# An expert loop on one core: VectorE alone splits the weights, conditional blocks get PSUM banks of their own, and token counts are read earlier

## The chip, the cores and the metric

The kernel runs on one NeuronCore of a Trainium2 chip. Its engines are TensorE (PE in the views; PEld is its weight load), VectorE (DVE), ScalarE (ACT), GpSimd (POOL) and the queue engine SyncE (SP). The metric is the device time of one execution in microseconds. It is taken from repeated runs; one further execution was recorded by the hardware profiler.

## What is computed

The program is two transformer blocks over 1024 tokens of width 1024. The first is a hybrid mixer with an MLP, the second a hybrid mixer with a mixture of experts, and only the mixture of experts is touched here. Each token chooses one of four groups and two of the four experts in it, so there are 16 experts and 2048 assignments, spread unevenly. All arithmetic of the experts is in float32:

```python
def expert_block(args):
    xb, e = args
    return (jax.nn.silu(xb @ w_gate[e]) * (xb @ w_up[e])) @ w_down[e]
...
out = jnp.zeros((n_tok, dm), ys.dtype).at[row_tok].add(ys)
```

`w_gate[e]` and `w_up[e]` are 1024x512, `w_down[e]` is 512x1024, so an expert has 6 MB of weights.

## The kernel before

**Precision by splitting.** Every float32 matrix that TensorE multiplies is cut into a high part (a cast to the fast format fp32r) and a low part (the value less the high part). A product is then three matmuls: high by high, high by low, low by high (`PASSES`, line 37; `products`, line 2071).

**The expert loop** is in `moe` (line 2007). The loop over `q` takes the 16 experts in a fixed order. An expert is three units `f`: f=0 and f=1 each compute one half of the gate and up products (`gate_up`), f=2 the down product (`down`). Tokens come in blocks of 128. Block b=0 always runs. Blocks b=1 and b=2 run inside `more` (lines 2123 and 2125) only if the expert's token count `c` is over 128 or 256; they reuse the weights already cut. More blocks than three go to `rest`, which this data does not enter. In the profiled execution the 16 experts run 3,1,1,1,3,2,1,1,2,1,1,1,2,2,1,1 blocks, 24 in all. I call them experts 1 to 16, and single-block, two-block and three-block experts.

**Weights.** SP loads 1 MB halves into seven `half` buffers (line 1998). One half is cut into two pieces `hl` of 128x1024 values, four pieces to a unit, twelve to an expert, in ten rotating buffers. A piece needs one cast on ScalarE (line 2052) and subtractions (line 2054). These are made in steps of half a piece: the cast and a 128x512 subtraction in one step, the second 128x512 subtraction in the next. The second subtraction of every other piece goes to GpSimd, so per expert VectorE makes 18 subtractions and GpSimd 6. The steps are called between the matmuls of block 0 of the unit before, so about six pieces are cut ahead.

**Activations.** Block b's tokens are gathered by GpSimd into `xg` (line 2030), turned by TensorE into `pl` (line 2040) and split by ScalarE and VectorE into `xT` (lines 2044 and 2045). A gate/up result in PSUM goes through a tanh on ScalarE (line 2085) and two operations on VectorE (lines 2086 and 2087) into `et`. TensorE turns `et` (line 2093), and lines 2095 and 2096 split it into `ehT`, the input of `down`. The results of `down` are copied to `yo` by ScalarE (line 2112) and VectorE (line 2113) and scattered by GpSimd (line 2115). Within `down` of block 0, TensorE also turns block 0 of the next expert.

**What sets the order.** The loop is under a manual schedule: each engine executes its instructions in the order in which the code was written, and in that order alone. PSUM tiles `pd` come from one pool of four rotating banks, used by conditional and unconditional blocks alike. A tile that a conditional block may have used is released when the reading engine has passed the branch, whether the block ran or not.

At the end of an expert every engine reads the next count and branches:

```python
if q < 15:
    c = count(q + 1)
    more(c, turn)
```

Of the kernel before, what the change touches and what calls it, by code (L numbers as in the profile page):

```python
# [44 lines left out]
class Kern:  # L45
# [1961 lines left out]
    def moe(s, hn_d, y_d):  # L2007
# [5 lines left out]
        with s.pool("me") as pl:  # L2013
# [12 lines left out]

            def fetch(e, b, full=False, to=None):

                o = 8 * e + b
                nc.gpsimd.indirect_dma_start(  # L2030
                    out=XG[b if to is None else to], out_offset=None, in_=hn_d,
                    in_offset=bass.IndirectOffsetOnAxis(ap=(ifull if full else ia)[:, o:o + 1], axis=0),
                    **({} if full else dict(bounds_check=T - 1, oob_is_err=False)))
# [13 lines left out]
            def split_of(x):  # L2047


                w = pl.tile([128, 2, 2, 512], F32R, name="hl", tag="hl", bufs=s.B_HL)  # L2050
                W.append(w)
                nc.scalar.copy(w[:, 0], x)  # L2052
                for i in range(2):
                    (nc.gpsimd if i and len(W) % 2 == 0 else V).tensor_sub(  # L2054
                        w[:, 1, i], x[:, i], w[:, 0, i].bitcast(F32))
                    if i == 0:
                        yield

            def cuts():

                while True:
                    n = len(W)
                    if n >= 192:
                        while True:
                            yield
                    yield from split_of(s.halves[n // 2][:, n % 2 * 2:n % 2 * 2 + 2])
                    yield
# [6 lines left out]
            def gate_up(b, w, f, step=lambda: None):  # L2074

                ps = s.psd()
                step()
                for k in range(8):
                    products(ps, XT[b][:, :, k], w, k, k == 0, k == 7)
                    if f == 1 and k == s.LEAD:  # L2080
                        turned(b, 0)
                    if k < 7:
                        step()
                g, x, t = ps[:, :256], ps[:, 256:], ET[b]
                nc.scalar.activation(t, g, AF.Tanh, scale=0.5)
                V.scalar_tensor_tensor(t, t, 1.0, g, op0=OP.add, op1=OP.mult)
                V.scalar_tensor_tensor(t, t, 0.5, x, op0=OP.mult, op1=OP.mult)
# [10 lines left out]
            def down(b, w, e, o, step=lambda: None, between=()):  # L2098

                Q = [s.psd(), s.psd()]  # L2100
                between = list(between)
                step()
                for n, (k, nh) in enumerate(((0, 0), (1, 0), (0, 1), (1, 1), (2, 0), (3, 0), (2, 1), (3, 1))):
                    products(Q[nh], EH[b][:, :, k], w, 2 * k + nh, k == 0, k == 3)
                    if n == s.T_B:
                        turned(b, 1)
                    if n > s.LEAD and between:
                        between.pop(0)()
                    if n < 7:
                        step()  # L2110
# [17 lines left out]
            def rest(q, b, c):  # L2128
# [3 lines left out]
                with tc.If(c > 128 * b):  # L2132
# [3 lines left out]
                    for f in range(3):  # L2136
                        w = []
                        for r in range(2):
                            x = s.half(e, f, r)
                            for i in range(2):  # L2140
                                s.run(split_of(x[:, 2 * i:2 * i + 2]))
                                w.append(W.pop())
# [7 lines left out]
            cut = cuts()  # L2150
            step = lambda: next(cut)
            with tc.manual_schedule(engines={POOL, PE, ACT, DVE}):
# [6 lines left out]
                for n in range(2 * (s.B_HL - 4)):  # L2159
                    step()  # L2160
                for q in range(16):
                    e = ORDER[q]
                    nxt = [lambda: turn(0, (0,)), lambda: turn(0, (1,))] if q < 15 else ()
                    for f in range(3):
# [10 lines left out]
                        if f < 2:  # L2175
                            more(c, lambda b: gate_up(b, w, f))
                        else:
                            more(c, lambda b: down(b, w, e, b))
                    if q < 15:
                        c = count(q + 1)  # L2180
                        more(c, turn)
# [96 lines left out]
```

## Time and profile before

| | us |
|---|---|
| median of 3 runs | 3620.5 (3619.45 to 3627.08) |
| the profiled execution | 3621.05 |
| its span, first to last instruction | 3619.2 |
| TensorE busy | 3371.8 (93% of the span) |
| VectorE busy | 2188.0 (60%) |
| ScalarE busy | 1197.8 (33%) |
| GpSimd busy | 897.1 (25%) |
| the expert loop in it | about 3028 to 3549, some 521 |

Nearly all of the program is bound by TensorE; the page's 40 slices show it 9 tenths busy or more in most of them, and lower ones in the last eight, where the expert loop lies. An engine's busy time does not tell by itself who waits for whom, so the rows used below are timelines of single experts and tables of waits. A timeline row is the start, the duration, the engine with the line, the operation, out and in, and the count of instructions merged into it; in brackets stands how long the engine was idle before and what ended that.

### The profile page before, as it was taken

Reading aid. Unit: us, or ns where it says so; the run is one execution under the profiler, and the core shown is the slowest. Engines: PE = TensorE matmul, PEld = TensorE weight load, DVE = VectorE, ACT = ScalarE, POOL = GpSimd, SP = SyncE. Lnnn points to the kernel's source line nnn. Section 1 sums busy time; section 2 is a strip of 40 time slices with the busy share of each in tenths; the row PEclk is TensorE's granted clock in tenths of the full one; section 3 lists DMA queues with packets and bytes.
Section 4 is the critical chain, followed back from the end, with each engine's and each line's share of the span. In section 5 each row is a group of like instructions: output and inputs, shape, how many; then the busy total and the mean of one; then the engine's idle time right before and its main releaser. Section 6 shows DMA issues by size and latency. Waiting matters only on the chain. (4 is left out here: it accounts for less than half of the span.)

```text
span 3619.2 us, 53008 instructions
## 1 busy us (share of the span) xinstructions
PE 3371.8 (93%) x20364; PEld 2907.8 (80%) x20364; DVE 2188.0 (60%) x4131; ACT 1197.8 (33%) x2013; POOL 897.1 (25%) x785
## 2 busy tenths in 40 slices
PE   7899999999999999999999999999999998898882
PEld 6889988899998998989977788888877786676671
DVE  5846666575566756666646844444556377757764
ACT  4433232322323223232333222222335333535552
POOL 1325223143232432323330000000120113524532
PEclk9999999999999999999999999999998998999995
DMA  3121111111121212111131221111252236847745
GB/s 102 55 61 44 50 41 50 47 43 51 49 56 36 52 42 58 45 47 43 53 136 63 82 70 48 49 47 47 82 148 70 75 111 228 272 164 240 265 165 200
DMA packets 311761, 324.60 MB, mean 90 GB/s; under 512 B 59340, under 2 KB 265784, under 8 KB 310800
## 3 DMA queue, kind: packets, MB, share of 16 engines
q1 hardware_dynamic: 245168, 258.53, 22.5%
q10 hardware_dynamic: 55936, 45.13, 4.4%
q0 software_dynamic: 10368, 17.10, 1.4%
q8 instruction: 180, 2.95, 0.3%
q14 instruction: 109, 0.89, 0.1%
HBM read 294.87 MB, written 46.47 MB: 94 GB/s over the span
## 5 line engine op out<-in xcount | busy, mean ns | idle before, releaser
L76 PE MATMUL pd<-wh,hT 128*128 128x256 f32 x6144 | 817.2, 289 | 1.9 <-DVE tg L600 1.9
L76 PEld LDWEIGHTS pd<-wh,hT 128*128 128x128 f32 x6144 | 768.0, 194 | 11.1 <-issue 2.7
L160 ACT CAST wh<-wr 128x512 fp32r<-128x512 f32 (+1 forms) x417 | 250.6, 601 | 941.6 <-PE pd L76 570.8
L76 PE MATMUL pd<-hT,wh 128*128 128x512 f32 x2256 | 562.0, 399 | 0.0
L161 DVE TENSOR_TENSOR wh<-wr,wh 128x512 fp32r<-128x512 f32 (+1 forms) x417 | 296.8, 718 | 414.9 <-ACT wh L160 413.6
L76 PEld LDWEIGHTS pd<-hT,wh 128*128 128x128 f32 x2256 | 413.6, 189 | 80.9 <-issue 0.2
L1171 PE MATMUL pd<-wh,uT 128*128 128x512 f32 x1536 | 360.2, 393 | 2.9 <-DVE acc L1179 1.9
L76 PE MATMUL pd<-h2T,wh 128*128 128x512 f32 x1536 | 352.8, 390 | 0.0
L1171 PEld LDWEIGHTS pd<-wh,uT 128*128 128x128 f32 x1536 | 286.9, 188 | 70.1 <-DVE acc L1179 8.3
L76 PEld LDWEIGHTS pd<-h2T,wh 128*128 128x128 f32 x1536 | 287.8, 188 | 60.5 <-issue 0.2
L2071 PE MATMUL pd<-hl,xT 128*128 128x512 f32 x1152 | 293.7, 413 | 30.6 <-DVEq L2123 23.3
L2071 PEld LDWEIGHTS pd<-hl,xT 128*128 128x128 f32 x1152 | 225.3, 200 | 89.1 <-ACT hl L2052 21.7
L2054 DVE TENSOR_TENSOR hl<-half,hl 128x512 fp32r<-128x512 f32 x288 | 259.0, 944 | 31.6 <-ACT hl L2052 26.7
L1179 DVE TENSOR_TENSOR acc<-acc,pd 128x512 f32<-128x512 f32 x224 | 146.8, 686 | 99.4 <-PE pd L1171 99.0
L2052 ACT CAST hl<-half 128x1024 fp32r<-128x1024 f32 x192 | 191.5, 1048 | 20.9 <-ACTq L2123 12.1
L2054 POOL TENSOR_TENSOR hl<-half,hl 128x512 fp32r<-128x512 f32 x96 | 139.4, 1462 | 222.0 <-ACT hl L2052 200.5
L1099 POOL TENSOR_TENSOR acc<-acc,gain 128x1024 f32<-128x1024 f32 x8 | 21.3, 2667 | 563.2 <-ACT hr L1098 563.1
L2071 PE MATMUL pd<-hl,ehT 128*128 128x512 f32 x576 | 151.5, 406 | 7.1 <-DVE ehT L2096 3.6
L76 PE MATMUL pd<-h3T,wh 128*128 128x512 f32 x552 | 140.1, 412 | 6.8 <-ACT bx L1457 5.5
L598 POOL TENSOR_SCALAR tg<-tg 128x256 f32<-128x256 f32 x96 | 86.1, 897 | 213.2 <-ACT tg L597 155.2
L135 POOL TENSOR_TENSOR orr<-orr,mhalf 128x4 f32<-128x4 f32 (+1 forms) x48 | 50.4, 1050 | 346.4 <-DVE orr L134 346.1
L76 PEld LDWEIGHTS pd<-h3T,wh 128*128 128x128 f32 x552 | 106.8, 196 | 35.3 <-ACT bx L1457 6.1
(582 smaller groups left out, 4934.5 us busy)
## 6 DMA issues: line engine op xcount, KB each, us to landing
wr<-in_w_in_dram SPq DMA_DIRECT2D x392, 128.0 KB, 2.3
half<-in_expert_w_gate_dram SPq DMA_DIRECT2D x64, 512.0 KB, 4.3
half<-in_expert_w_up_dram SPq DMA_DIRECT2D x64, 512.0 KB, 5.6
half<-in_expert_w_down_dram SPq DMA_DIRECT2D x32, 1024.0 KB, 5.0
wr<-in_w_up_dram SPq DMA_DIRECT2D x64, 256.0 KB, 2.7
wr<-in_w_down_dram SPq DMA_DIRECT2D x64, 256.0 KB, 2.5
wr<-in_w_in_dram SPq DMA_DIRECT2D x56, 256.0 KB, 2.8
x_d<-xr SPq DMA_DIRECT2D x16, 512.0 KB, 2.6
```

The lines of the kernel that those rows point to most:

```text
L76: return s.nc.tensor.matmul(out, a, b, start=start, stop=stop, **kw)
L135: nc.gpsimd.tensor_tensor(out, out, s.mhalf[:, :n], op=OP.pow)
L160: s.nc.scalar.copy(wv[:, 0], rv)
L161: s.nc.vector.tensor_sub(wv[:, 1], rv, wv[:, 0].bitcast(F32))
L598: nc.gpsimd.tensor_scalar(t[:, :, 128:], t[:, :, 128:], 1.0, None, op0=OP.add)
L1099: nc.gpsimd.tensor_mul(row, row, gpost)
L1171: nc.tensor.matmul(ps, ups[fb][k][:, a, t * 128:(t + 1) * 128], p[k][:, b, 0, :], start=(n == 0), stop=(n == 6 * len(fbs) - 1))
L1179: nc.vector.tensor_add(o, o, ps)
L2052: nc.scalar.copy(w[:, 0], x)
L2054: (nc.gpsimd if i and len(W) % 2 == 0 else V).tensor_sub(w[:, 1, i], x[:, i], w[:, 0, i].bitcast(F32))
L2071: nc.tensor.matmul(ps, lhs[:, a], w[i // 2][:, c, i % 2], start=first and n == 0, stop=last and n == 2)
```

## The change

Three edits, all in the expert loop.

1. **Subtractions.** A step is now a whole piece: one cast of 128x1024 and one subtraction of 128x1024 on VectorE. GpSimd makes none. Four steps fall into a unit, before every second product group. Twelve subtractions per expert replace 18 on VectorE and 6 on GpSimd.
2. **Banks.** The pool's four `pd` banks are taken once and given fixed parts, with the banks `ps` and `pt` besides. Block 0 uses banks 0 and 1 for gate/up and 2 and 3 for down. Conditional blocks use 4 and 5 only.
3. **Counts.** The next expert's count is read after unit f=0. The conditional turning of the next expert's blocks 1 and 2 stands before the conditional `down` blocks of this expert, no longer after them.

```diff
+            BANKS = [s.psd() for _ in range(4)] + [s.pss(), s.pst()]
...
                 w = pl.tile([128, 2, 2, 512], F32R, name="hl", tag="hl", bufs=s.B_HL)
-                W.append(w)
                 nc.scalar.copy(w[:, 0], x)
-                for i in range(2):
-                    (nc.gpsimd if i and len(W) % 2 == 0 else V).tensor_sub(
-                        w[:, 1, i], x[:, i], w[:, 0, i].bitcast(F32))
-                    if i == 0:
-                        yield
...
+                V.tensor_sub(w[:, 1], x, w[:, 0].bitcast(F32))
+                return w
+
+            def step():
+
+                n = len(W)
+                if n < 192:
+                    W.append(split_of(s.halves[n // 2][:, n % 2 * 2:n % 2 * 2 + 2]))
...
-                ps = s.psd()
-                step()
+                ps = BANKS[f] if b == 0 else BANKS[3 + b]
                 for k in range(8):
+                    if k % 2 == 0:
+                        step()
                     products(ps, XT[b][:, :, k], w, k, k == 0, k == 7)
...
-                Q = [s.psd(), s.psd()]
+                Q = BANKS[2:4] if b == 0 else BANKS[4:6]
...
+                    if n % 2 == 0:
+                        step()
                     products(Q[nh], EH[b][:, :, k], w, 2 * k + nh, k == 0, k == 3)
...
-                for n in range(2 * (s.B_HL - 4)):
+                for n in range(s.B_HL - 4):
                     step()
...
                             more(c, lambda b: gate_up(b, w, f))
+                            if f == 0 and q < 15:
+                                c1 = count(q + 1)
                         else:
+                            if q < 15:
+                                more(c1, turn)
                             more(c, lambda b: down(b, w, e, b))
-                    if q < 15:
-                        c = count(q + 1)
-                        more(c, turn)
+                    c = c1
```

On TensorE, at the end of expert 2, the kernel before has the last `down` matmuls of block 0, the conditional `down`, the count, the conditional turning and the next expert's first matmul (`pd` with a number is a PSUM tile, `ehT1` and `xT0` are the inputs of block 1 and block 0):

```order
L2071 MATMUL pd_27540<-hl_27427,ehT0_26764 128x512 x3
L2123 COMPARE_AND_BRANCH
L2071 MATMUL pd_27612<-hl_27331,ehT1_26765 128x512 x3
...
L2123 UNCONDITIONAL_BRANCH
L2149 TENSOR_LOAD cnt_26700
L2123 COMPARE_AND_BRANCH
L2040 MATMUL pl_27700<-ident_86,xg1_26759 128x128 x4
...
L2071 MATMUL pd_27738<-hl_27442,xT0_26761 128x512 x6
```

With the change the same place reads:

```order
L2064 MATMUL pd_26775<-hl_27004,ehT0_26764 128x512 x3
L2114 COMPARE_AND_BRANCH
L2042 MATMUL pl_27178<-ident_86,xg1_26759 128x128 x4
...
L2114 COMPARE_AND_BRANCH
L2064 MATMUL ps_26776<-hl_26891,ehT1_26765 128x512 x3
...
L2114 UNCONDITIONAL_BRANCH
L2064 MATMUL pd_26772<-hl_27018,xT0_26761 128x512 x6
```

The turning moved ahead of the conditional `down`, the count is gone from here, and the conditional block now writes `ps_26776` and `pt_26777` while the next expert's first product has a bank of its own, `pd_26772`.

On VectorE, in units f=1 and f=2 of block 0 of an expert, the conditional parts left out, the kernel before has:

```order
L2054 TENSOR_TENSOR hl<-half,hl 128x512 x3
L2086 SCALAR_TENSOR_TENSOR et_26767<-et_26767,pd 128x256
L2087 SCALAR_TENSOR_TENSOR et_26767<-et_26767,pd 128x256
...
L2054 TENSOR_TENSOR hl<-half,hl 128x512 x2
L2096 TENSOR_TENSOR ehT_26764<-pl,ehT_26764 128x256
L2054 TENSOR_TENSOR hl<-half,hl 128x512 x2
L2045 TENSOR_TENSOR xT_26761<-pl,xT_26761 128x512
L2054 TENSOR_TENSOR hl<-half,hl 128x512
L2045 TENSOR_TENSOR xT_26761<-pl,xT_26761 128x512
L2054 TENSOR_TENSOR hl<-half,hl 128x512
L2113 COPY yo_26770<-pd 128x512
```

With the change:

```order
L2053 TENSOR_TENSOR hl<-half,hl 128x1024 x2
L2078 SCALAR_TENSOR_TENSOR et_26767<-et_26767,pd 128x256
L2079 SCALAR_TENSOR_TENSOR et_26767<-et_26767,pd 128x256
...
L2053 TENSOR_TENSOR hl<-half,hl 128x1024
L2088 TENSOR_TENSOR ehT_26764<-pl,ehT_26764 128x256
L2053 TENSOR_TENSOR hl<-half,hl 128x1024 x2
L2047 TENSOR_TENSOR xT_26761<-pl,xT_26761 128x512 x2
L2053 TENSOR_TENSOR hl<-half,hl 128x1024
L2104 COPY yo_26770<-pd 128x512
```

The operations on `et`, `ehT`, `xT` and `yo` keep their places; the subtractions between them became fewer and wider, and the two on `xT` are now back to back. ScalarE's row of casts is the same in both kernels.

## Rows read from the trace of the kernel before

**Rows 1.** Waits of TensorE in the loop: us in total, times, longest.
```profile
PE pd L2071 <- DVEq L2123: 23.3, 9, 2.9
PE pl L2093 <- DVEq L2123: 12.3, 9, 1.9
PE pl L2040 <- DVEq L2123: 7.3, 3, 2.8
```

**Rows 2.** Stretch table, nine single-block experts with a successor: columns, one, sum.
```profile
core 0: us, PE busy (x) PEld busy (x) DVE busy (x) ACT busy (x) POOL busy (x), PEclk, DMA share, GB/s
...
3134.59:3159.11 24.52, 20.37 (x84) 15.48 (x85) 19.23 (x27) 13.49 (x18) 13.18 (x10) 0.92 0.96 314
...
sum 222.30, PE 178.88 PEld 135.66 DVE 180.81 ACT 132.96 POOL 115.39; mean PE 19.88 PEld 15.07 DVE 20.09 ACT 14.77 POOL 12.82
```

**Rows 3.** TensorE's timeline: end of expert 3, start of 4; expert 7 from 3255.72.
```profile
3130.08 1.64 PE L2071 MATMUL pd<-hl,ehT 128*128 128x512 f32 x6
3134.59 10.47 PE L2071 MATMUL pd<-hl,xT 128*128 128x512 f32 x36 [2.87 <-DVEq L2123]
...
3255.72 5.69 PE L2071 MATMUL pd<-hl,xT 128*128 128x512 f32 x24 [1.95 <-DVEq L2123]
...
3270.96 0.41 PE L2093 MATMUL pl<-ident,et 128*128 128x128 f32 x2 [1.68 <-DVEq L2123]
...
3274.78 1.64 PE L2071 MATMUL pd<-hl,ehT 128*128 128x512 f32 x6
3279.29 5.71 PE L2071 MATMUL pd<-hl,xT 128*128 128x512 f32 x24 [2.87 <-DVEq L2123]
```

**Rows 4.** VectorE's timeline at the end of expert 3 and start of 4.
```profile
3131.58 0.68 DVE L2045 TENSOR_TENSOR xT<-pl,xT 128x512 fp32r<-128x512 f32 x1
3132.18 1.61 DVE L2054 TENSOR_TENSOR hl<-half,hl 128x512 fp32r<-128x512 f32 x1
3133.71 0.68 DVE L2113 COPY yo<-pd 128x512 f32<-128x512 f32 x1
3135.33 3.72 DVE L2054 TENSOR_TENSOR hl<-half,hl 128x512 fp32r<-128x512 f32 x6 [0.94 <-ACT hl L2052]
```

**Rows 5.** GpSimd's timeline there: a subtraction, and a gather's descriptors.
```profile
3131.98 1.26 POOL L2054 TENSOR_TENSOR hl<-half,hl 128x512 fp32r<-128x512 f32 x1 [2.08 <-ACT hl L2052]
...
3138.44 1.47 POOL L2030 DMA_INDIRECT xg<-hn_d,ia  x1 [0.31 <-issue]
```

**Rows 6.** Stretch table of line 2054 alone, the same nine experts: sum.
```profile
sum 222.30, DVE 145.69 POOL 77.55; mean DVE 16.19 POOL 8.62
```

**Rows 7.** Line 665 by source, a 128x1024 operation of VectorE: ns min/median/max.
```profile
L665 DVE TENSOR_TENSOR aq<-aq,af x8: 1206/1213/3432, 96.5 to 1600.6; 128x1024 f32<-128x1024 f32 x8
```

**Rows 8.** Line 2149 by source, TensorE's queue reading a count: ns min/median/max.
```profile
L2149 PEldq TENSOR_LOAD <-cnt x16: 302/310/1162, 3021.7 to 3525.2; - x16
```

**Rows 9.** Stretch table, the four two-block experts: the sum.
```profile
sum 162.18, PE 149.57 PEld 118.92 DVE 94.89 ACT 72.74 POOL 59.15; mean PE 37.39 PEld 29.73 DVE 23.72 ACT 18.19 POOL 14.79
```

**Rows 10.** TensorE's timeline: start of expert 5; two-block expert 14; start of expert 16.
```profile
3159.11 1.94 PE L2040 MATMUL pl<-ident,xg 128*128 128x128 f32 x8 [2.82 <-DVEq L2123]
...
3163.28 20.29 PE L2071 MATMUL pd<-hl,xT 128*128 128x512 f32 x84
...
3463.43 1.06 PE L2040 MATMUL pl<-ident,xg 128*128 128x128 f32 x8 [1.43 <-DVEq L2125]
3465.03 11.17 PE L2071 MATMUL pd<-hl,xT 128*128 128x512 f32 x48 [0.53 <-ACT xT L2044]
...
3497.01 4.37 PE L2071 MATMUL pd<-hl,ehT 128*128 128x512 f32 x18
...
3527.91 8.59 PE L2071 MATMUL pd<-hl,xT 128*128 128x512 f32 x24 [2.87 <-DVEq L2123]
```

**Rows 11.** The load queue SP in the loop: its longest wait; landing times of halves.
```profile
SPq L1998 <- DVE hl L2054: 310.7, 75, 13.4
...
DMA to landing us min/median/max: 3.3/5.0/10.2
```

More of the change, by code (lines that the diff above doesn't have):

```diff
@@ L2050, in split_of @@
                 w = pl.tile([128, 2, 2, 512], F32R, name="hl", tag="hl", bufs=s.B_HL)
-                W.append(w)
                 nc.scalar.copy(w[:, 0], x)
-                for i in range(2):
-                    (nc.gpsimd if i and len(W) % 2 == 0 else V).tensor_sub(
-                        w[:, 1, i], x[:, i], w[:, 0, i].bitcast(F32))
-                    if i == 0:
-                        yield
[L2059 to L2067, printed above, removed]
+                V.tensor_sub(w[:, 1], x, w[:, 0].bitcast(F32))
[4 more added lines that the diff above has]
+                    W.append(split_of(s.halves[n // 2][:, n % 2 * 2:n % 2 * 2 + 2]))
             def products(ps, lhs, w, i, first, last):
@@ L2081, in gate_up @@
                         turned(b, 0)
-                    if k < 7:
-                        step()
                 g, x, t = ps[:, :256], ps[:, 256:], ET[b]
@@ L2098, in down @@
             def down(b, w, e, o, step=lambda: None, between=()):
-                Q = [s.psd(), s.psd()]
+                Q = BANKS[2:4] if b == 0 else BANKS[4:6]
                 between = list(between)
-                step()
                 for n, (k, nh) in enumerate(((0, 0), (1, 0), (0, 1), (1, 1), (2, 0), (3, 0), (2, 1), (3, 1))):
+                    if n % 2 == 0:
+                        step()
                     products(Q[nh], EH[b][:, :, k], w, 2 * k + nh, k == 0, k == 3)
@@ L2108, in down @@
                         between.pop(0)()
-                    if n < 7:
-                        step()
                 yo = YO[b % 2]
@@ L2139, in rest @@
                             x = s.half(e, f, r)
-                            for i in range(2):
-                                s.run(split_of(x[:, 2 * i:2 * i + 2]))
-                                w.append(W.pop())
+                            w += [split_of(x[:, 2 * i:2 * i + 2]) for i in range(2)]
                         if f < 2:
@@ L2149, in moe @@
             count = lambda q: nc.values_load(s.cnt[0:1, ORDER[q]:ORDER[q] + 1], min_val=0, max_val=1024)
-            cut = cuts()
-            step = lambda: next(cut)
             with tc.manual_schedule(engines={POOL, PE, ACT, DVE}):
```

## The prediction

> **What bounds the kernel now.** The change lies in the expert loop, about 521 of 3619 us. The chain of waits that ended last covers only the last 40 us, behind the loop, and tells nothing of it. So I read first TensorE's waits in the loop, then the loop expert by expert in the stretch table, then the timelines of the engines around one wait.
>
> The waits [rows 1] have one releaser, VectorE's queue passing the branch at line 2123: 23.3 us before an expert's first product, 7.3 us before the turning at its start, 12.3 us before the transposes in `down`. They belong to the single-block experts. Ten of 16 are such, and the nine with a successor take 222.30 us, 24.70 each, with TensorE busy 19.88 and VectorE 20.09 [rows 2]. Neither engine is full: they wait for each other in turn. A two-block expert needs twice the products for the same weights, and there VectorE is well ahead.
>
> One seam shows how. TensorE ends expert 3 at 3131.72 and starts expert 4 at 3134.59 [rows 3]. What the first product reads was ready earlier: the last subtraction on `xT` ended at 3132.26. VectorE still made a subtraction until 3133.79 and the copy of `yo` until 3134.39, then passed the branch [rows 4]. So TensorE waited for a bank that a conditional block, which did not run, might have used. That subtraction took 1.61 us where the others take 0.62 from start to start (3.72 for six), since GpSimd subtracted at the same time [rows 4, 5].
>
> The clock follows. The start of expert 4, behind 2.87 us of idleness, shows 36 products in 10.47 us; expert 7, with no dip behind its 1.95 us, 24 in 5.69, which would be 8.6 for 36 [rows 3]. Expert 4's granted clock is 0.92 [rows 2], so part of it ran at 1.2 GHz, the rest at 2.4. Not every long gap is followed by a dip (expert 8 starts with 24 in 5.71 behind 2.87 [rows 3]).
>
> **The banks, for a single-block expert.** TensorE's own work is read from expert 7: 3255.72 to 3276.42 at full clock is 20.70, less its wait of 1.68 in `down`, 19.02 [rows 3]. Of the 2.87 at the seam there remain the branches and what is left until `xT` is split, 0.54 in expert 3 (3131.72 to 3132.26) for its second half, which the first product does not need; I take 0.3. TensorE alone would then need 19.3. The Trainium skill (Perfetto Trace Analysis, Optimization Strategy) says that the same gap repeating on the engine that should be full can mean too little SBUF or PSUM for the next tile. Read so, the whole 2.87 would go and the expert would take 19.0 at best, 2.7 us less over nine; the rows keep the 0.3.
>
> **The subtractions.** VectorE is busy 20.09 us in such an expert, 16.19 of it in 18 subtractions [rows 2, 6]; 3.90 is other work and stays. The trace has no 128x1024 subtraction into fp32r, the nearest is line 665: median 1.213 us, slowest 3.432 [rows 7]. I take the median, because with GpSimd's subtractions gone nothing shown here disturbs it: a gather's descriptors on GpSimd (3138.44) left the six subtractions beside them at 0.62 [rows 4, 5]. Back to back they overlap by some 0.06 (0.68 long, 0.62 apart), so twelve cost 12 x 1.15 = 13.8. With 3.9 that is 17.7; empty stretches at branches, the count read (0.31, as on TensorE's queue [rows 8]) and waits for a cast add 1.0 to 1.5: 18.7 to 19.2. ScalarE's work, 14.77 [rows 2], is unchanged and stays hidden. GpSimd keeps only gathers and scatters.
>
> Both engines now need about 19.3. They still meet once per expert: the `et` of f=1 must be ready when six `down` products are done, and it stands behind up to one whole subtraction, 1.2 us long and no longer 0.68. The wait there is 12.3 over nine today, 1.37 each [rows 1]; with VectorE no longer behind I leave 0.5. So 19.8 per expert, a saving of 24.70 - 19.8 = 4.9, nine times: **44.1 us**. No dip is left in this number; today's dips are within the 24.70.
>
> **The other experts.** Two-block expert 14 at full clock took 36.35 from its first product to its end (3465.03 to 3501.38) [rows 10]. With 0.3 of branches it is 36.65, and 1.1 more for turning block 1 (1.06) where that lies in its stretch, which is so in three of four: 4 x 36.65 + 3 x 1.1 = 149.9, against 162.18 [rows 9]: **12.3 us**. The gap behind such an expert goes for the same reason. Three-block expert 5 spends 4.17 us (3159.11 to 3163.28) on turning 16 tiles that cost 1.06 per eight at full clock; with the gap ahead of it gone: **2.1 us**. Expert 1 starts cold and does not change. The last expert's first unit, 8.59 for 24 products against 5.69: **2.9 us** [rows 3, 10].
>
> **The count and the turning.** The count read moves from a place where TensorE waited anyhow to one behind a running unit; it costs at most 0.31 x 15 = 4.7 us if nothing hides it, and I take 0, since the queue reads ahead of the running products. It must be below the 0.3 that I leave at each seam to matter. Behind the moved turning the conditional `down` is queued on TensorE; the turning needs `pl` tiles that VectorE frees with `xT`, a wait of some 0.5 at six experts at most, and its gather is as old as before. It counts within the 1.1. At the loop's start the first subtraction is 1.21 instead of 0.69 long: 0.5 lost.
>
> **Sum.** 44.1 + 12.3 + 2.1 + 2.9 - 0.5 = 60.9 us. The profiled execution took 3621.05, so 3621.05 - 60.9 = 3560.15, **3560**. The median of the runs is 0.55 lower, which I neglect.
>
> **Rivals.**
>
> *VectorE stays behind.* The wider subtraction delays whatever stands behind it: the 1.37 in `down` stay and grow by 1.21 - 0.68 = 0.53 to 1.9, and the 0.54 for `xT` stays. Then 19.0 + 0.3 + 1.9 + 0.5 = 21.7, a saving of 3.0 x 9 = 27.0 and with the other 16.8 together 43.8: **3577**. For it: the two engines are level in my sum, so any slip falls on TensorE. Against: VectorE loses 2.4 us of work per expert (16.19 - 13.8). The Trainium skill (Perfetto Trace Analysis, Optimizing Scalar/DVE Operations) speaks for this rival: where VectorE is not full but causes bubbles elsewhere, its instructions should be broken up; this change does the opposite.
>
> *The loads become the bound.* In expert 4 the DMA engines were busy 0.96 and moved 314 GB/s [rows 2], so full they would move some 327. A single-block expert needs 6.3 MB of weights, 0.5 of tokens, 0.5 of results: 7.3 MB, 22.4 us. Saving 2.3 x 9 + 16.8 = 37.5: **3584**. Against: SP waits 310.7 us for VectorE to free a buffer, and a half lands within 10.2 us [rows 11], while seven halves, more than one expert's six, lie ahead; three single-block experts in a row would fall behind by 3 x 2.6 = 7.8 us and live off that lead. The Trainium skill (DMA: Bandwidth & Descriptors, Specifications) gives about 358 GB/s as a core's limit from HBM; by it an estimate is 20.4 us per expert, 18 us better over nine than by the row.
>
> *The banks free nothing*, because something else in VectorE's queue holds TensorE at the seam. Only the subtractions' 2.4 x 9 = 21.6 are won: **3599**.
>
> *Slower.* The disturbance of VectorE is not GpSimd's subtraction but something that stays. At each of the 12 places the wide subtraction then costs twice the 1.61 of [rows 4], 3.2 us, near the slowest of line 665, 3.43 [rows 7]: 12 x 3.15 + 3.9 + 1.3 = 43.0 per single-block expert, 18.3 x 9 = 165 lost, 16.8 won: **3769**. It decides from 24.70 + 16.8/9 = 26.6 per expert, that is a subtraction of 1.84 us. Against: the undisturbed six beside the gathers.
>
> **Chances.** Forecast 0.62; VectorE behind 0.17; loads 0.09; banks free nothing 0.06; slower 0.06. What a measurement can tell from no change is about 0.2%, 7 us. Faster by more than that take the first three cases and part of the fourth: 0.90; within it 0.04; slower 0.06. The range: at best TensorE alone bounds the single-block experts and the seam costs nothing, 19.0, which saves 0.8 x 9 = 7.2 more, 3553, with 3 us for what else is small: 3550. Above it reaches over the first two rivals, to 3586.
>
> **What would show it.** Right: TensorE's waits for VectorE's branch ahead of line 2064's first product near zero; single-block experts at 19 to 20.5 us; granted clock 1.00 in them; wide subtractions at 1.21 us with nothing on GpSimd beside them. Wrong: wide subtractions of 1.5 us and more; a wait before the transposes in `down` of 1.5 us or more in every single-block expert; ScalarE waiting for landing halves in the third of a row of single-block experts; dips that stay without the seam's gap.

## The result and the profile after

The changed kernel takes 3572.0 us (median of 4 runs, 3570.4 to 3578.0) against 3620.6 for the kernel before: 48.6 us less, ratio 0.9865 with a 95% interval of 0.9848 to 0.9882. The forecast was 3560, in a range of 3550 to 3586. So the sign and the range held, and the size was 12 us too large.

The profiled execution took 3570.43 us (span 3568.6), 50.6 less than the one of before. Read by the loop alone, from the first product of expert 1 to the last of expert 16, it is 518.3 us before (3030.42 to 3548.73) and 471.4 after (3027.63 to 3499.05): 46.9 less. The other 3.7 lie outside the loop, where nothing was changed: the loop of these profiles starts anywhere between 3025 and 3035. The loop's length is the steadier measure, and the same kernel profiled again gave 470.6. I use it below; but each is the loop of one execution, and a difference of 1 us tells nothing.

TensorE's waits in the loop, us in total, times, longest. The 23.3, 12.3 and 7.3 of [rows 1] have gone. What is left is mostly short gaps behind branches, 29 of them adding up to 16.8 us (the first three rows), and 3.3 us in all before the transposes in `down`:

```profile
PE pd L2064 <- PEq L2114: 8.6, 15, 0.8
PE pd L2064 <- PEq L2116: 4.9, 8, 0.8
PE pd L2064 <- ACTq L2116: 3.3, 6, 0.8
PE pl L2085 <- DVEq L2114: 3.3, 13, 0.4
```

The stretch table, columns as in [rows 2]: two of the nine single-block experts with a successor and the sum of the nine, the sum of the four two-block experts, and the loop as one stretch. The stretches are laid as in [rows 2, 9]; a conditional turning counts to the stretch in which it stands, so that for expert 14 now counts to expert 13, and that for expert 6 to expert 5, as before:

```profile
3103.56:3123.88 20.32, 18.74 (x84) 14.34 (x85) 18.20 (x22) 14.89 (x20) 5.84 (x4) 1.00 0.98 326
3123.88:3143.45 19.57, 18.59 (x85) 14.44 (x85) 17.73 (x21) 14.14 (x19) 5.83 (x4) 1.00 1.02 357
...
sum 180.93, PE 168.18 PEld 129.42 DVE 158.36 ACT 129.96 POOL 51.48; mean PE 18.69 PEld 14.38 DVE 17.60 ACT 14.44 POOL 5.72
...
sum 158.67, PE 146.84 PEld 114.82 DVE 93.24 ACT 72.67 POOL 25.62; mean PE 36.71 PEld 28.70 DVE 23.31 ACT 18.17 POOL 6.41
...
3033.00:3499.00 466.00, 437.56 (x1983) 343.07 (x1981) 317.07 (x397) 252.82 (x348) 88.06 (x65) 1.00 0.68 232
```

A single-block expert went from 24.70 to 20.10 us, VectorE's work in it from 20.09 to 17.60, and the granted clock is 1.00 over the whole loop behind its start. Expert 3 on TensorE:

```profile
3103.56 5.72 PE L2064 MATMUL pd<-hl,xT 128*128 128x512 f32 x24 [0.57 <-PEq L2114]
3109.91 2.98 PE L2064 MATMUL pd<-hl,xT 128*128 128x512 f32 x12 [0.63 <-PEq L2114]
...
3117.85 0.41 PE L2085 MATMUL pl<-ident,et 128*128 128x128 f32 x2 [0.24 <-DVEq L2114]
...
3123.88 5.71 PE L2064 MATMUL pd<-hl,xT 128*128 128x512 f32 x24 [0.56 <-PEq L2114]
```

The seam is 0.57 where [rows 3] had 2.87. But there is now a gap of 0.63 between f=0 and f=1, where the kernel before had none or 0.15. On VectorE the seam of the same expert reads as follows; its copy of `yo` ends at 3125.35, 1.5 us after TensorE has started the next expert, so the copy no longer holds it:

```profile
3121.93 1.34 DVE L2047 TENSOR_TENSOR xT<-pl,xT 128x512 fp32r<-128x512 f32 x2
3123.53 1.23 DVE L2053 TENSOR_TENSOR hl<-half,hl 128x1024 fp32r<-128x1024 f32 x1 [0.26 <-ACT hl L2052]
3124.67 0.68 DVE L2104 COPY yo<-pd 128x512 f32<-128x512 f32 x1
```

All 192 wide subtractions, ns min/median/max. None is disturbed:

```profile
L2053 DVE TENSOR_TENSOR hl<-half,hl x192: 1210/1221/1299, 3027.6 to 3489.8; 128x1024 fp32r<-128x1024 f32 x192
```

Where the missing 14 us of the loop (60.9 forecast, 46.9 measured) sit, in the forecast's own terms:

| term | before | after | saved | forecast |
|---|---|---|---|---|
| nine single-block experts | 222.30 | 180.93 | 41.4 | 44.1 |
| four two-block experts | 162.18 | 158.67 | 3.5 | 12.3 |
| turning ahead of expert 5 | 4.17 | 4.32 | -0.1 | 2.1 |
| expert 16 | 20.82 | 17.88 | 2.9 | 2.9 |
| expert 1 | 54.73 | 55.77 | -1.0 | -0.5 |
| expert 5, products | 54.10 | 53.86 | 0.2 | 0 |

### The profile page after: what moved, and what is told of

Same layout as the page of the kernel before. It is cut to its first block, busy times and chain, and to the rows that moved or that the text cites. A ratio compares the mean times of both kernels' runs of the same rounds, so it can differ in the third digit from the quotient of the medians.

```text
span 3568.6 us, 52664 instructions
## 1 busy us (share of the span) xinstructions
PE 3352.3 (94%) x20364; PEld 2891.2 (81%) x20364; DVE 2157.2 (60%) x4035; ACT 1198.0 (34%) x2013; POOL 775.7 (22%) x689
## 5 line engine op out<-in xcount | busy, mean ns | idle before, releaser
L2053 DVE TENSOR_TENSOR hl<-half,hl 128x1024 fp32r<-128x1024 f32 x192 | 226.4, 1222 | 35.0 <-ACT hl L2052 28.1
L2064 PE MATMUL pd<-hl,xT 128*128 128x512 f32 x768 | 189.6, 399 | 18.7 <-PEq L2114 8.2
L2064 PEld LDWEIGHTS pd<-hl,xT 128*128 128x128 f32 x768 | 142.3, 190 | 58.8 <-issue 18.6
L954 DVE TENSOR_TENSOR prd<-Xt,nb 128x8 f32<-128x8 f32 (+30 forms) x248 | 107.4, 433 | 11.3 <-DMA nb<-nb_d 5.9
L2106 POOL DMA_INDIRECT y_d<-yo,slots x24 | 32.6, 1358 | 368.3 <-DVEq L2114 169.9
```

The source lines that it names most:

```text
L954: nc.vector.tensor_mul(pr[:, :, :i], X[:, :, :i], nb[:, None, :i, i].to_broadcast([128, 8, i]))
L2053: V.tensor_sub(w[:, 1], x, w[:, 0].bitcast(F32))
L2064: nc.tensor.matmul(ps, lhs[:, a], w[i // 2][:, c, i % 2], start=first and n == 0, stop=last and n == 2)
L2106: d = nc.gpsimd.indirect_dma_start(out=y_d, out_offset=bass.IndirectOffsetOnAxis(ap=ir[:, o:o + 1], axis=0), in_=yo, in_offset=None, bound ...
```

## The experiments

Line numbers differ a little from kernel to kernel. "Loop" is the length defined above.

### One edit at a time

**Banks alone.** The kernel before with only this:

```diff
+            BANKS = [s.psd() for _ in range(4)] + [s.pss(), s.pst()]
-                ps = s.psd()
+                ps = BANKS[f] if b == 0 else BANKS[3 + b]
-                Q = [s.psd(), s.psd()]
+                Q = BANKS[2:4] if b == 0 else BANKS[4:6]
```

> The kernel before with edit 2 alone (the fixed banks), subtractions, count and turning as before. Read by the loop, from the first product to the last: before 518.3 us, changed 471.4. Theory A (the seam's wait was the bank, but VectorE's own work of 20.09 plus 1.0 to 1.5 of empty stretches is then the bound of a single-block expert): 21.3 to 21.6 us per single-block expert, no waits for VectorE's branch ahead of the first product, waits of over 1 us before the transposes in down stay: loop about 480. Rival F (VectorE doesn't matter once the banks are free): singles 20.1 to 20.5, loop 470 to 475. Rival G (banks free nothing, VectorE's queue holds TensorE otherwise): loop above 510.

Measured: loop 512.5, ratio 0.9997 (0.9981 to 1.0012). My theory of 480 was wrong by 32 us, and G had the number but not the reason. Expert 11 on TensorE:

```profile
3362.55 5.70 PE L2073 MATMUL pd<-hl,xT 128*128 128x512 f32 x24 [0.97 <-PEq L2125]
...
3379.88 0.66 PE L2095 MATMUL pl<-ident,et 128*128 128x128 f32 x2 [3.73 <-DVEq L2125]
```

The banks do free the seam, 0.97 instead of 2.87. The time returns a few microseconds later: the wait before the transposes in `down` is 3.73 in this expert, the longest of them. Over the loop the waits are:

```profile
PE pl L2095 <- DVEq L2125: 15.8, 9, 3.7
PE pd L2073 <- PEq L2125: 13.0, 17, 2.1
PE pd L2073 <- DVE ehT L2098: 10.4, 6, 2.3
```

Before, the wait ahead of the transposes was 12.3 us in all and the one ahead of the first product 23.3 [rows 1]; products that wait for `ehT` lost 3.6 before and lose 10.4 now. What the seam gave, `down` took: the nine single-block experts took 222.30 us before and take 223.45. The clock paid too: 0.87 was granted in expert 11's stretch, where before had 0.94. The waits were one debt of VectorE, paid in several places.

**Subtractions alone.** The kernel before with edit 1 only; the banks rotate, and count and turning stand at the expert's end.

> The kernel before with edit 1 alone (wide subtractions on VectorE), banks, count and turning as before. Theory A: the seam's wait stays, because the bank is still released by VectorE passing the branch behind its copy of yo; it shortens from 2.87 to some 1.9 us since VectorE has less to do, and the wait in down falls to 0.3: singles about 22.6, loop about 496 (before 518.3). Rival H (the subtractions alone held TensorE): seam under 1 us, singles near 20.3, loop 472 to 476.

Measured: loop 491.4, ratio 0.9934 (0.9914 to 0.9953), close to the 496 of theory A. Here the opposite wait goes: 0.20 in `down`, and 2.24 stay at the seam, because the bank is still released behind the copy of `yo`:

```profile
3371.67 0.41 PE L2083 MATMUL pl<-ident,et 128*128 128x128 f32 x2 [0.20 <-DVEq L2112]
...
3379.36 0.93 PE L2062 MATMUL pd<-hl,xT 128*128 128x512 f32 x3 [2.24 <-DVEq L2112]
```

**Without edit 3**, so both of the above together.

```diff
                             more(c, lambda b: gate_up(b, w, f))
-                            if f == 0 and q < 15:
-                                c1 = count(q + 1)
                         else:
-                            if q < 15:
-                                more(c1, turn)
                             more(c, lambda b: down(b, w, e, b))
-                    c = c1
+                    if q < 15:
+                        c = count(q + 1)
+                        more(c, turn)
```

> The changed kernel without edit 3: count read and conditional turning stand at the expert's end again, after the conditional down. Theory A: the gap between f=0 and f=1 falls to about 0.15 (0.42 in two-block experts), the seam of a single-block expert grows from 0.57 to about 0.95, since the read is exposed there, so that single-block experts stay at 20.1; in two-block experts the gap of 0.32 ahead of the conditional down and the 0.29 behind it go, some 3 us over four: 3569, so edit 3 gave nothing. Rival D, that edit 3 is worth what the early read saves: the seam grows by over 1 us because the engines must meet there again: 3580 or more.

Measured: loop 474.3, median 3573.8. The edits' shares of the loop are thus 5.8 us for the banks alone, 26.9 for the subtractions alone, 44.0 for both, 46.9 with edit 3: the two first are worth 11.3 more together than apart. The medians, each against the kernel before on its own chip, say 1.1, 25.1 and 41.5, so 15 more together; for the banks alone they show no change, and the profiled execution of that kernel was one of its fastest. I had expected edit 3 to give nothing, or 8 us and more by rival D; it gave about 3 by the loops, while the ratios, 0.9889 (0.9868 to 0.9910) and 0.9865, are not told apart. The first of the rows below is the seam, grown to 0.98 as expected, since the count is now read there; the second is what I had not seen, three turnings that wait 2.2 us each for VectorE when they stand behind the conditional `down`:

```profile
3100.93 4.36 PE L2064 MATMUL pd<-hl,xT 128*128 128x512 f32 x18 [0.98 <-PEq L2114]
...
PE pl L2042 <- DVEq L2114: 6.6, 3, 2.2
```

### What held VectorE

**A quarter back to GpSimd**, in the changed kernel:

```diff
-                V.tensor_sub(w[:, 1], x, w[:, 0].bitcast(F32))
+                if len(W) % 2 == 0:
+                    V.tensor_sub(w[:, 1], x, w[:, 0].bitcast(F32))
+                else:
+                    V.tensor_sub(w[:, 1, 0], x[:, 0], w[:, 0, 0].bitcast(F32))
+                    nc.gpsimd.tensor_sub(w[:, 1, 1], x[:, 1], w[:, 0, 1].bitcast(F32))
```

> The changed kernel with the second half of every other piece given to GpSimd again (so 6 wide and 6 half subtractions on VectorE and 6 on GpSimd in an expert); banks and count as changed. Theory A: beside GpSimd's subtraction VectorE's run about twice as long, the wide ones up to 2.5 us and more in place of 1.22, so that VectorE's busy time does not fall by the 6 x 0.54 = 3.2 us of work taken from it; it stays at 17 to 19.5 per single-block expert, TensorE waits for it in down at 0.3 to 1: loop 472 to 480. Rival K (no disturbance: GpSimd's help is a gain): VectorE at 14.4, loop 470 to 471.4. Rival L (the disturbance alone made the time before): singles back above 22, loop over 490.

Measured: loop 513.7, ratio 0.9984, which is rival L; theory A had the disturbance and far too small a price for it. Giving VectorE less to do brought most of the old time back, with the banks and the early counts in place: over the loop its subtractions were busy 263.9 us (162.8 wide, 101.1 half) instead of 226.4. Expert 11, first VectorE, then GpSimd:

```profile
3378.22 4.99 DVE L2054 TENSOR_TENSOR hl<-half,hl 128x1024 fp32r<-128x1024 f32 x1 [0.52 <-ACT hl L2052]
...
3375.21 1.85 POOL L2032 DMA_INDIRECT xg<-hn_d,ia  x1 [0.30 <-issue]
3377.08 5.04 POOL L2057 TENSOR_TENSOR hl<-half,hl 128x512 fp32r<-128x512 f32 x4
```

GpSimd is busy with three gathers in f=0, so its subtractions pile up and run four in a row, 3377.08 to 3382.12. VectorE's wide subtraction starts in the middle of this and ends at 3383.21, 1.09 us behind GpSimd: that is nearly the 1.22 that it takes alone, so it stood still until they were done. Expert 11's transposes in `down` waited 3.46 us for it. The Trainium skill (SBUF — State Buffer, SBUF: two separate sides) says that VectorE with two SBUF inputs and GpSimd lock a shared port pair for a whole instruction and the other blocks; the 4.99 us row agrees, and VectorE did not get in between the four here.

**A subtraction that nobody needs.** That kernel leaves a doubt: the pieces might merely have been late, since GpSimd made them late. So here VectorE keeps all its work, and GpSimd adds a subtraction that no product waits for:

```diff
                 V.tensor_sub(w[:, 1], x, w[:, 0].bitcast(F32))
+                if len(W) % 2:
+                    nc.gpsimd.tensor_sub(DUM, x[:, 1], w[:, 0, 1].bitcast(F32))
```

> The changed kernel, complete, with one thing added: for every other piece GpSimd also makes the 128x512 subtraction of its second half into a tile that nothing reads. No product waits for it, and VectorE's own work is unchanged. With GpSimd's subtractions counting (the kernel that gave GpSimd a quarter again) the loop was 513.7 us against 471.4. Theory A (GpSimd's subtraction stops VectorE's beside it): the loop is longer than with the quarter given away, since VectorE keeps the whole work: over 514, perhaps 540 (six stops of 0.9 to 1.3 us in an expert whose VectorE has 2.5 us to spare, and four of them in a row behind the gathers), wide subtractions up to 4 to 5 us. Rival O (the pieces that GpSimd made were merely late): the loop stays at 471 to 474, wide subtractions at 1.22.

Measured: loop 536.6, median 3635.2, ratio 1.0040 (1.0029 to 1.0051): slower than the kernel before. The group of wide subtractions (busy us, mean ns), and TensorE's wait in `down`:

```profile
L2054 DVE TENSOR_TENSOR hl<-half,hl 128x1024 fp32r<-128x1024 f32 x190 | 301.3, 1628 | 32.2 <-ACT hl L2053 24.6 <-DVEq L2117 3.4 <-DMA half<-in_expert_w_up_dram 2.7
...
PE pl L2088 <- DVEq L2117: 39.2, 13, 4.0
```

The mean rises from 1222 to 1628 ns with no work added to VectorE, and TensorE waits 39.2 us in `down` instead of 3.3. Lateness of GpSimd's pieces is ruled out as the cause: no product uses them here. SyncE does wait for GpSimd to have read a half (136.1 us in the loop), but ScalarE waits for landing halves only 4.1 us in all. The longest wide subtraction is 3.00 us, not the 4 to 5 that I expected. In expert 3, VectorE, then GpSimd:

```profile
3127.58 5.20 DVE L2054 TENSOR_TENSOR hl<-half,hl 128x1024 fp32r<-128x1024 f32 x2 [1.02 <-ACT hl L2053]
3133.04 4.17 DVE L2054 TENSOR_TENSOR hl<-half,hl 128x1024 fp32r<-128x1024 f32 x2
...
3128.14 7.99 POOL L2056 TENSOR_TENSOR dum<-half,hl 128x512 f32<-128x512 f32 x4
```

Here VectorE did get in between four GpSimd subtractions: two of its own were done at 3132.78, and the last at 3137.21, 1.08 us behind GpSimd's end at 3136.13. GpSimd is slowed in turn, 7.99 us for four instead of 5.04. Why the engines took turns here and not in expert 11 above stays open.

**Two half subtractions.** The changed kernel with each wide subtraction cut in two:

```diff
-                V.tensor_sub(w[:, 1], x, w[:, 0].bitcast(F32))
+                for i in range(2):
+                    V.tensor_sub(w[:, 1, i], x[:, i], w[:, 0, i].bitcast(F32))
```

> The changed kernel with each 128x1024 subtraction made as two of 128x512 back to back on VectorE. It adds 12 x (2 x 0.62 - 1.15) = 1.1 us of VectorE's work to a single-block expert, 17.6 to 18.7 of its 20.1. Theory A (TensorE bounds, VectorE has slack): loop within 2 us of 471.4, the wait before the transposes in down stays near 0.24. Rival I (VectorE is level with TensorE): 1.1 x 9 and more: 481. Rival J (the Trainium skill, Perfetto Trace Analysis, Optimizing Scalar/DVE Operations: break up instructions that cause bubbles; by that rule shorter pieces let et through sooner): the wait in down goes, 0.24 x 9 = 2.2 us less: 469.

Measured: loop 473.1, 1.7 more than the changed kernel, ratio 0.9897 (0.9866 to 0.9927); TensorE's wait in `down` grows a little, from 3.3 us in all:

```profile
PE pl L2086 <- DVEq L2115: 5.0, 13, 0.6
```

So the width of the subtractions hardly matters, and VectorE has slack: 13.0 us more work for it over the loop (226.4 to 239.4 us busy with the subtractions) cost 1.7 to 2.5 us of time. What mattered in edit 1 is that GpSimd stopped. The rule on breaking up instructions (the Trainium skill, Perfetto Trace Analysis, Optimizing Scalar/DVE Operations) would allow a gain here; there was none, since little was left to wait for.

### What the early count costs

**Count ahead of the branch:**

```diff
-                            more(c, lambda b: gate_up(b, w, f))
                             if f == 0 and q < 15:
                                 c1 = count(q + 1)
+                            more(c, lambda b: gate_up(b, w, f))
```

> The changed kernel with one line moved: the count of the next expert is read ahead of the conditional gate/up blocks of f=0, no longer behind them. Theory A: in the changed kernel the read costs TensorE about 0.4 us at each of 15 experts, because it stands behind the semaphore instruction at the end of the skipped block, which waits for the last product; ahead of the branch the queue reads it while products still run. The gap between f=0 and f=1 then falls from 0.55-0.63 to about 0.15 us in single-block experts and from 0.78 to about 0.42 in two-block ones, 15 x 0.4 = 6 us less: 3566. Rival B: the read holds TensorE's queue for its 0.31-0.38 us wherever it stands: the gap moves into f=0, and the time stays at 3572.

In the changed kernel, expert 3, TensorE's queue (xcount, ns min/median/max, first and last start) shows the read at 3109.5, for 0.38 us, behind the semaphore instruction at 3109.3 that closes the skipped block; the last product had ended at 3109.28:

```profile
L2138 PEldq TENSOR_LOAD <-cnt x1: 380/380/380, 3109.5 to 3109.5; - x1
...
L2114 PEldq EVENT_SEMAPHORE  x3: 51/51/51, 3103.0 to 3109.3; - x3
```

With the read moved, expert 2 runs from f=0 into f=1 without a gap, 36 products in a row:

```profile
3081.26 8.72 PE L2064 MATMUL pd<-hl,xT 128*128 128x512 f32 x36
```

Loop 467.5, 3.9 less than the changed kernel and 3.1 less than its second profile. The median, 3567.8, is a ratio of 0.9869 (0.9847 to 0.9891) on its chip, which is not told apart from the changed kernel's 0.9865; the gain is read from the loop and its gaps alone. Theory A expected 6 us less and got the mechanism right, rival B is out. Single-block experts gained 0.40 each, two-block ones 0.34; expert 5 was 1.3 us longer in this profile, for which I have no cause.

**Count twice.** The same read written twice in a row, to price one.

> The changed kernel with the count read twice in a row at the same place. Theory A (the read is exposed there in full): the gap between f=0 and f=1 grows by 0.31 to 0.38 us at 15 experts, to about 0.93 in single-block ones: 4.7 to 5.7 us more, 3577. Rival C (the gap is the branch's, the read hides in it): gap and time unchanged, 3572.

This run does not answer its question. Only 16 reads stand on TensorE's queue, with 15 semaphore instructions at the same line: the first of each pair, which has no user, is not read there. Loop 473.0, the gap in expert 2 0.71 instead of 0.55; ratio 0.9890 (0.9874 to 0.9907).

**Turning ahead of the last product group of `down`:**

```diff
-                    nxt = [lambda: turn(0, (0,)), lambda: turn(0, (1,))] if q < 15 else ()
+                    nxt = [lambda: turn(0, (0,)), lambda: turn(0, (1,)), lambda: more(c1, turn)] if q < 15 else ()
...
-                            if q < 15:
-                                more(c1, turn)
                             more(c, lambda b: down(b, w, e, b))
```

> The changed kernel with the conditional turning moved in front of the last product group of block 0's down (behind the unconditional turning), so that two skipped blocks no longer stand in a row at the seam. Theory A: the seam of nine single-block experts falls from 0.57 to about 0.15 to 0.3, and the 0.6 us around the conditional down of two-block experts goes; the skipped block now costs about 0.1 us inside down: some 3 to 4 us less, 3568.5. Rival E: a skipped block costs the same wherever it stands, since it drains TensorE each time: the gap moves, the time stays at 3572.

Measured: loop 469.6, 1.8 less; median 3569.8, ratio 0.9877 (0.9861 to 0.9894). For single-block experts rival E is right: in expert 2 the seam closes, but the six products ahead of it take 2.03 instead of 1.64, so the gap only moved. The gain is in the two-block experts (154.96 to 152.60, first product to first product).

```profile
3100.33 2.03 PE L2064 MATMUL pd<-hl,ehT 128*128 128x512 f32 x6
3102.51 2.78 PE L2064 MATMUL pd<-hl,xT 128*128 128x512 f32 x11
```

**Both, beside the changed kernel on the same chip:**

> The changed kernel itself once more, beside the two below, since single profiles of one kernel start the loop at different times. Its loop, from the first product to the last, was 471.4 us; expected 471.4 within 1 us, and a median within 0.2% of 3572.

> The changed kernel with both moves tried apart: the count is read ahead of the conditional gate/up of f=0, and the conditional turning stands in front of the last product group of block 0's down. Apart they made the loop 467.6 and 469.6 us, against 471.4. Theory A: they touch different gaps and add: loop 465.8, 5.6 us less than the changed kernel. Rival M (the loads are level with TensorE in rows of single-block experts, where they moved up to 357 GB/s): part of it is lost to waits of ScalarE for landing halves; loop 467.5 or more.

The changed kernel again: loop 470.6, median 3571.8, ratio 0.9866. With both moves: loop 463.4, median 3567.0, ratio 0.9855 (0.9835 to 0.9875). By the loops they add, and gave 2.4 more than theory A had; the ratios' intervals overlap. The loads took nothing back.

**One skipped block fewer.** The conditional turning goes into the conditional block that f=0 of its own expert has anyway; the gathers move from f=0 to f=1, so that they don't overwrite what is still to be turned:

```diff
-                        if f == 0 and q < 15:
+                        if f == 1 and q < 15:
                             for b in range(NB):
                                 fetch(ORDER[q + 1], b)
...
-                            more(c, lambda b: gate_up(b, w, f))
                             if f == 0 and q < 15:
                                 c1 = count(q + 1)
+                            if f == 0 and q:
+                                more(c, lambda b: (turn(b), gate_up(b, w, f)))
+                            else:
+                                more(c, lambda b: gate_up(b, w, f))
                         else:
-                            if q < 15:
-                                more(c1, turn)
                             more(c, lambda b: down(b, w, e, b))
```

> The changed kernel with the count read first, and the conditional turning of blocks 1 and 2 moved into the conditional blocks of f=0 of their own expert, so that a single-block expert skips three conditional blocks and not four; the gathers move from f=0 to f=1. Theory A: each skipped block costs TensorE 0.3 to 0.45 us of drain, branch and semaphore; nine single-block seams fall from 0.57 to 0.15, and the 0.6 around the conditional down of three two-block experts goes: 5.5 us less than the 467.6 of the kernel with the count first; against that each of 5 turnings stands behind f=0 and its products wait for the split behind VectorE's queued subtraction, some 1 us more each: loop 465 to 468. Rival N (that wait is 2 us or more at each, since a wide subtraction is always ahead of the split): loop 470 to 476.

Measured: loop 460.0, better than the 465 to 468 expected; median 3562.5, ratio to before 0.9839 (0.9821 to 0.9857). This is the fastest of all: 11 us less in the loop than the changed kernel and 9.3 in the medians of the same chip, though the two ratios' intervals overlap. The price that I had put at 1 us each came out as 4.4 us over five experts, 0.9 each. Expert 6 shows one of the cheaper ones, 0.24 and 0.30 for the split of block 1, and a conditional `down` with no gap ahead of it. Expert 5's two turnings with their waits took about 3.4 us, against 4.32 in the changed kernel. The rest of what came out better than expected is not traced to a row.

```profile
3202.39 1.03 PE L2042 MATMUL pl<-ident,xg 128*128 128x128 f32 x8
3203.66 0.73 PE L2064 MATMUL ps<-hl,xT 128*128 128x512 f32 x2 [0.24 <-ACT xT L2046]
3204.70 5.27 PE L2064 MATMUL ps<-hl,xT 128*128 128x512 f32 x22 [0.30 <-DVE xT L2047]
...
3229.29 1.53 PE L2064 MATMUL ps<-hl,ehT 128*128 128x512 f32 x6
```

## Why the prediction was right, and where it was off

**Single-block experts: right, 41.4 of 44.1.** The expert came out at 20.10 where 19.8 was forecast. The subtraction (1.213 forecast, 1.221 measured) and VectorE's work (17.7, measured 17.60) were right, the clock's dips are gone, and VectorE has slack, as the halved subtractions show. Three small terms were off. The count was put at 0 and costs 0.40. The seam was put at 0.3 and is 0.57: two skipped blocks stand there in a row. The wait in `down` was put at 0.5 and is 0.24. That the last two nearly cancel is luck.

**The count: the step failed.** "I take 0, since the queue reads ahead of the running products." The queue does read ahead, but not past the semaphore instruction that ends a skipped block, which comes once the last product is done. Moving the read ahead of the branch removed the gap. The bound that I gave, 0.31 x 15 = 4.7, was slightly too small too: moving the read gained 0.40 in each of nine experts and 0.34 in each of four, 5.0 us without the two three-block ones.

**Two-block experts: the largest miss, 3.5 of 12.3.** The 36.65 was read from expert 14 of before, and the step took it that the expert itself would not change. It did, by the edit; two rows of before, then after:

```profile
3476.62 3.04 PE L2071 MATMUL pd<-hl,xT 128*128 128x512 f32 x12 [0.42 <-ACTq L2125]
3494.03 3.01 PE L2071 MATMUL pd<-hl,ehT 128*128 128x512 f32 x12
...
3434.51 3.00 PE L2064 MATMUL pd<-hl,xT 128*128 128x512 f32 x12 [0.78 <-PEq L2116]
...
3453.84 1.63 PE L2064 MATMUL ps<-hl,ehT 128*128 128x512 f32 x6 [0.32 <-PEq L2114]
3455.76 0.41 PE L2085 MATMUL pl<-ident,et 128*128 128x128 f32 x2 [0.29 <-DVEq L2114]
...
3460.73 5.78 PE L2064 MATMUL pd<-hl,xT 128*128 128x512 f32 x24 [0.42 <-PEq L2116]
```

In expert 14 after, the count adds 0.36 between f=0 and f=1 (0.78 where before had 0.42). The skipped turning, now ahead of the conditional `down`, adds 0.32 before it and 0.29 at its transposes; in before the first six products of that block followed with no gap, in one row of 12 with those of block 0. I had asked what is queued behind the turning, and answered it only for the case in which the turning runs. Where it does run, it costs its 1.04 us and a gap of 0.8 in experts 9 and 13, not 1.1 in all; a gap of 0.53 behind it could have been read in [rows 10]. Of the 8.8 us that are missing, some 6.1 are in the four experts themselves, 1.8 in the turnings, and 0.9 is one gap that the trace puts down to nothing, in the middle of f=0 of expert 13. With the turning out of that place (turned ahead of the last product group) the four experts gained 2.4 us, without edit 3 they gained nothing net, since then the turning waited instead. The gap in expert 13 stays unexplained.

**Expert 5's turning: a price read at the wrong place.** I took the 4.17 us as slow transposes:

```profile
3143.45 1.03 PE L2042 MATMUL pl<-ident,xg 128*128 128x128 f32 x8
3146.35 1.27 PE L2042 MATMUL pl<-ident,xg 128*128 128x128 f32 x8 [1.86 <-issue]
3146.32 0.42 PEld L2042 LDWEIGHTS pl<-ident,xg 128*128 128x128 f32 x4 [2.07 <-issue]
3146.96 0.42 PEld L2042 LDWEIGHTS pl<-ident,xg 128*128 128x128 f32 x4 [0.23 <-issue]
...
3143.82 1.23 DVE L2053 TENSOR_TENSOR hl<-half,hl 128x1024 fp32r<-128x1024 f32 x1 [0.25 <-ACT hl L2052]
3144.96 0.68 DVE L2104 COPY yo<-pd 128x512 f32<-128x512 f32 x1
3145.57 1.28 DVE L2047 TENSOR_TENSOR xT<-pl,xT 128x512 fp32r<-128x512 f32 x2
```

At full clock eight transposes do take 1.03, but the second eight start 2.90 us behind the first, where before it was 2.54 (3159.11 and 3161.65). Block 2 needs the two `pl` tiles that block 1 has just filled. VectorE splits them only behind a wide subtraction and the copy of `yo`; the two splits end at about 3146.25 and 3146.85, and each time four transposes follow within 0.11 us. So the limit was VectorE's split, and faster transposes only wait longer. The last experiment agrees: there the products of block 1 stand between the two turnings, and the second eight have no gap ahead of them.

**Expert 16** was right at 2.9; the start lost 1.0 instead of 0.5; the changed kernel's second profile has 55.24 for that stretch, so half of the 1.0 lies within what single profiles differ by.

**The rivals.** *VectorE stays behind* fell: 0.24 in `down`, and 1.7 us for the halved subtractions. Its 3577 lies nearer to the 3572 measured than the forecast's 3560, but by the chance of terms that have nothing to do with it: the missing time is in the two-block experts, the turning and the count. *The loads* fell too, though the 327 GB/s on which it rested was too low: expert 4 moved 357, and 371 in the last experiment. The Trainium skill's 358 GB/s for a core (DMA: Bandwidth & Descriptors, Specifications) was thus passed here; the measurement decides. *The banks free nothing* was wrong for the change as a whole and right for that edit alone, as the first experiment shows. My sum gave the seam to the banks and the work to the subtractions as if each could be had by itself; it came out because both were there. *Slower* had the right mechanism in the wrong place: VectorE is stopped for whole instructions, but by GpSimd's subtraction and not by something that stays. With six such subtractions to an expert left in, useless as they were, the kernel was indeed slower than before. One slip in the chances: *the banks free nothing*, at 3599, is 21 us faster than before, so its whole 0.06 belonged to "faster".

## What to carry to other kernels

When two engines wait for each other in turn, price the waits as one debt: closing one of them alone may only move the time to the next meeting point, so ask of each edit what it is worth without the others. Before giving an idle engine a share of the work, look for its instructions beside stretched ones of the engine that is to be relieved: here help from GpSimd cost VectorE more than it took off. And a branch whose block does not run is not free: put reads ahead of it, and let work that is conditional on the same count share one block.

## What was not expected of the hardware

- VectorE's 128x1024 subtraction, 1.22 us alone, took 4.99 us beside four GpSimd subtractions in a row, and ended 1.09 us behind the last: a stop, not a slower pace. In another run the two engines took turns, four wide subtractions against four of GpSimd's, the last ending 1.08 us behind.
- A skipped conditional block cost TensorE 0.15 us in expert 15 before, but 0.39 in the middle of `down`, and what stands on its queue behind it is exposed: 0.4 us for a register read; two skipped blocks in a row make a gap of 0.57.
- The loads reached 357 GB/s in a single-block expert, 1.02 of the DMA engines' time by the profile, and 371 in the fastest kernel; TensorE did not wait for them.
